# Two-layer decoder trunk: first up weights through the ring of two, an earlier load order where the up phase hands over to the down phase, and two operand or engine changes in attention and output projection

## The chip, the cores and the metric

The kernel runs on one core of a Trainium2 chip. The metric is the device time of one execution in microseconds, the median of several runs. An execution is profiled as well; its trace gives start, duration and releaser of every instruction on each engine: TensorE (PE, matmuls), VectorE (DVE), ScalarE (ACT), GpSimd (POOL) and SyncE (SP, which here only issues DMAs).

## The reference, cut to what matters

```python
for l in range(2):                                   # DEPTH
    h = rms_norm(x, norm1[l]);  proj = h @ w_in[l]   # S = D = 1024, fp32
    a_in, b_in, q, k, v = ...                        # 256 | 512 | 512 | 512 | 512 columns
    ya = pool_mixer(a_in, pool_w[l], pool_scale[l])
    yb = spatial_gate(gelu(b_in), sg_norm[l], sg_w[l], sg_b[l])
    yc = stick_breaking_attention(q, k, v)           # 8 heads of 64
    x = x + concat(ya, yb, yc) @ w_out[l]
    h = rms_norm(x, norm2[l])
    x = x + square(relu(h @ w_up[l])) @ w_down[l]    # 1024 -> 4096 -> 1024
return rms_norm(x, final_norm)

# stick breaking, per query row, causal, with z = q.k / 8
a[j] = sigmoid(z[j]) * prod over j' > j of (1 - sigmoid(z[j']))
out  = a @ v
```

## The kernel before, in words

Activations are kept transposed, as tiles of 128 features by 512 tokens, in two halves of the tokens (c = 1 and 0). Every fp32 product is made of three matmuls on fp32r operands: a value is split into a rounded part h (a cast on ACT, line 155) and a rest l = value - h (a subtraction on DVE, line 156), and h·h, l·h and h·l are added in PSUM (lines 243, 248, 249). In the trace a name such as hT, lT or wh, wl is such a pair.

A layer runs through these stages: input projection with the two small mixers, attention, output projection, up phase, down phase.

**Attention.** For each head and block of 128 queries, `sticks` takes one or two PSUM tiles z of query-key products (ring of three). ACT makes s = sigmoid(-z) (L426) and a = sigmoid(z) (L427), DVE runs a product scan over s in place (L431), and POOL multiplies a by the shifted s (L434). `attend` transposes a on PE, splits the result (L456 on ACT, L458 on DVE) and multiplies with v.

**Output projection.** PE makes 16 outputs `po` per layer. For each, `second` adds the residual on DVE (xa, L870), stores it, and hands the square to POOL's running sum for the norm (L187 on `rbc`). Then `scaled` makes from four outputs the blocks that the up phase multiplies: B11, B21, B22 (h on ACT, l on DVE, L882) and the mixed ones T1 to T4 (t on DVE, L887; h = cast on ACT, L888; l = t - h on POOL, L889).

**Up phase.** The MLP is done by a seven-product scheme on 2x2 blocks (`STEPS`: B11, B21, T2, T1, T3, B22, T4 against A11, A12, S2, S1, S3, S4, A22; PSUM banks X, Y, Z). There are 16 pairs of hidden blocks, `fp`, of seven steps. Each step is 12 matmuls. Its results are relu-squared and written to DRAM: B11 and B21 as finished h/l pairs, the T blocks and B22 raw (`hd_T`, `hd_B`). `weight_steps` brings the next pair's weights: two DMAs of 512 KB into `rt` and `raw` (L823), then splits and sums (`s`, `tmp`, wh, wl, uh, ul, vh, vl). `rt` is a tile of pool `mw`, which is opened after the output projection's pools have closed; `raw` is a ring of two in the pool that lives all the time.

**Down phase.** Groups of two `fp`, each with two halves `u` of seven steps; a step is 2 x 6 matmuls, and every result is added into a tile `acc` on DVE (L1110). A hidden block comes by DMA: finished pairs directly, raw blocks into the ring `hr` of three tiles (L946) followed by a split (L155, L156). At the change of phase the last `fp` steps already load the blocks of group 0 (`b_next`), the rest is loaded in group 0's first steps.

What sets the order: the program is written in Python order and a scheduler that simulates the engines interleaves it. `early(n)` raises priority for evacuations; in the up phase `queue` pins the order on ACT, DVE and POOL to the order of writing. Tile pools with rings make a writer wait for the last reader of the tile it replaces. SP issues DMAs in order, and one whose tile isn't free holds the next ones up.

Of the kernel before, what the change touches and what calls it, by code (L numbers as in the profile page):

```python
# [7 lines left out]
F32 = mybir.dt.float32  # L8
# [6 lines left out]
P = 128  # L15
# [65 lines left out]
def trunk_kernel(tc, xT, w_in, w_out, w_up, w_down, pool_w, sgw, sgb, sgn, cst, outT):  # L81
# [8 lines left out]
    with ExitStack() as ctx:  # L90
# [236 lines left out]
        for l in range(DEPTH):  # L327
# [8 lines left out]
            with (  # L336
# [72 lines left out]
                def sticks(pr, h, i):  # L409

                    c, o = divmod(i, 4)
                    qs = slice(o * P, (o + 1) * P)
                    prev, res = None, {}
                    for kc in ((0, 1) if c == 0 else (1,)):
                        lo = o * P if kc == c else 0
                        w = CH - lo
                        z = ap.tile([P, CH], F32, tag="z", name=nm("z"), bufs=3)
                        kt = kx[pr, h, kc]
                        nc.tensor.matmul(z[:, 0:w], qh[pr, h, c][:, qs], kt[:, lo:CH], start=True, stop=False)
                        mm = nc.tensor.matmul(z[:, 0:w], ql[pr, h, c][:, qs], kt[:, lo:CH], start=False, stop=prev is not None)  # L420
                        if prev is None:
                            mm = nc.tensor.matmul(z[:, 0:P], identr, maskr, start=False, stop=True)
                        last_qk[0] = mm.ins.name
                        s = t512("s", NS, F32, at)
                        a = t512("a", NA, F32, at)
                        nc.scalar.activation(s[:, lo:CH], z[:, 0:w], AF.Sigmoid, scale=-ISQ)  # L426
                        nc.scalar.activation(a[:, lo:CH], z[:, 0:w], AF.Sigmoid, scale=ISQ)  # L427
                        if prev is not None:
                            nc.gpsimd.tensor_mul(a[:, 0:1], a[:, 0:1], prev[:, CH - 1 : CH])
                        sl = s[:, lo:CH]  # L430
                        nc.vector.tensor_tensor_scan(  # L431
                            sl, sl, sl, 1.0 if prev is None else prev[:, CH - 1 : CH], ALU.mult, ALU.bypass
                        )
                        nc.gpsimd.tensor_mul(a[:, lo + 1 : CH], a[:, lo + 1 : CH], s[:, lo : CH - 1])  # L434
                        prev = s
                        res[kc] = a
                    return res
# [359 lines left out]
                b = "T1" if b == "B12" else b  # L797
                return t512("h" + b, 4, F32R, pool), t512("l" + b, 4, F32R, pool)

            def weight_steps(srcs, n, out, eng="pool"):  # L800

# [12 lines left out]
                    return two  # L816

                def load():
                    r["top"] = mw.tile([P, D], F32, tag="rt", name=nm("rt"), bufs=1)
                    r["low"] = per.tile([P, D], F32, tag="raw", name=nm("raw"), bufs=2)  # L820
                    raws = r["top"], r["low"]
                    for raw, src in zip(raws, srcs):
                        nc.sync.dma_start(raw.rearrange("p (f c) -> p f c", f=src.shape[1]), src)  # L823
                    r["a1"], r["a2"] = (x.rearrange(turns, n=n, k=2) for x in raws)
# [42 lines left out]
            def second(m, c, ps):  # L867
# [9 lines left out]
                def scaled(b, src, in1, op):  # L877
# [8 lines left out]
                    t = t512("xt", 3, F32, xs_)  # L886
                    nc.vector.scalar_tensor_tensor(out=t, in0=src, scalar=g, in1=in1, op0=ALU.mult, op1=op)  # L887
                    nc.scalar.copy(h, t)  # L888
                    nc.gpsimd.tensor_sub(lo, t, h.bitcast(F32))  # L889
                    return t  # L890

                if not low and c == 1:
# [45 lines left out]
                acc_[m, c] = pool.tile([P, CH], F32, name=nm("acc"))  # L938
                nc.sync.dma_start(acc_[m, c], xmid[m, c])

            def raw_block(fp, b):

                if b in STORED:
                    return None
                raw = t512("hr", 3, F32, mw)
                nc.sync.dma_start(raw, hid[fp, b])  # L946
                return raw

# [8 lines left out]
                return h, lo  # L957

            a_next = {}
            for step in weight_steps(*up_blocks(0), a_next).values():  # L960
                step()


            with tc.tile_pool(name=f"mu{l}", bufs=1, reuse_waits="tile") as mu:
# [8 lines left out]
                for fp in range(NFP):  # L973
# [51 lines left out]
                    for step in range(len(STEPS)):  # L1025
# [1 line left out]
                        ps = banks[bank]  # L1027
                        b = STEPS[step][3]
                        if (fp, step) == (NFP - 2, 3):
                            raws = {"T2": [raw_block(p, "T2") for p in range(2)], "T1": [raw_block(0, "T1")]}  # L1030
                        if (fp, step) == (NFP - 1, 3):
                            raws["T1"].append(raw_block(1, "T1"))
                        if (fp, step) == (NFP - 1, 4):
                            raws["T3"] = [raw_block(p, "T3") for p in range(2)]
                        if step == 5 and fp == 0:
                            rms(1, 0)
                            rms_done = True
# [27 lines left out]
                        if not classic:  # L1065
# [3 lines left out]
                                mixed("T3", "B22", "B12", nc.vector.tensor_sub)  # L1069
                            elif step == 6:  # L1070
                                mixed("T4", "B21", "T2", nc.vector.tensor_sub)
                        if fp == NFP - 1 and step < 5:
                            for p in range(2):
                                b_next[p][b] = load_block(p, b, raws[b][p] if b in raws else None)
                for k in sorted(left):
# [28 lines left out]
            with tc.tile_pool(name=f"md{l}", bufs=1, reuse_waits="tile") as md:  # L1104
# [8 lines left out]
                for mc in ((3, 0), (2, 1), (3, 1)):  # L1113
# [1 line left out]


                first_acc = {
                    k: [(4 + i + q, c) for q in range(2)] for k, i, c in ((1, 0, 1), (2, 0, 0), (3, 2, 0), (4, 2, 1))
                }
                for g in range(n_groups):  # L1120
                    bs, b_next = b_next, [{}, {}]
                    for u in range(2):
# [6 lines left out]
                        for step in range(len(STEPS)):  # L1129
# [23 lines left out]
                            if g == u == 0:  # L1153
                                for mc in first_acc.get(step, []):
                                    load_acc(*mc, md)
                                if step < 2:
                                    for p in range(2):
                                        bs[p][STEPS[step + 5][3]] = load_block(p, STEPS[step + 5][3])
                            elif g < n_groups - 1:
                                for p in range(2) if g == 0 else (u,):  # L1160
                                    b_next[p][b] = load_block(2 * g + 2 + p, b)
# [122 lines left out]
```

## Time and profile before

| | |
|---|---|
| median of 3 runs | 2274.09 us (2271.59 to 2276.8) |
| the profiled execution's own time | 2273.57 us |
| its span, first to last instruction | 2271.7 us |
| PE busy | 2144.4 us, 94% of the span |
| DVE / POOL / ACT busy | 1830.7 (81%) / 1070.8 (47%) / 952.0 us (42%) |
| mean granted TensorE clock | 0.976 of full speed |
| stages, layer 0 | attention about 40 to 380 us, output projection to 460, up phase to about 803, down phase after that |
| stages, layer 1 | attention about 1160 to 1480 us, up phase from about 1590, down phase from about 1918 |

The page gives an engine's busy time as a sum over its instructions, also where instructions overlap a little in their pipelines. A row of a timeline is one instruction or several alike (xN): start, duration, engine and line, tiles written and read, and in brackets how long the engine had been idle before it and which instruction or DMA ended that. In the table by form, a row is a group of equal instructions with count, busy time and mean ns of one. SPq is the queue of SP, that is, the issue of DMAs.

### The profile page before, as it was taken

How to read it: one execution, taken by the hardware profiler on the slowest of the kernel's cores; microseconds unless marked ns; L12 is line 12 of the kernel's file. 1: busy time of each engine (PE TensorE's matmuls, PEld its weight loads, DVE VectorE, ACT ScalarE, POOL GpSimd, SP SyncE). 2: the span in 40 equal slices, each digit the busy share in tenths (PEclk: the TensorE clock that was granted, in tenths of full speed). 3: DMA queues.
4: the chain of work that ended last, by engine and by line, in shares of the span. 5: the costliest groups of instructions: out<-in, count | busy, mean ns of one | idle time of the engine just before them, and what ended most of it. 6: DMA issues, size and time to landing. Idle time of an engine off the chain costs nothing. (4 is left out here: it accounts for less than half of the span.)

```text
span 2271.7 us, 30343 instructions
## 1 busy us (share of the span) xinstructions
PE 2144.4 (94%) x10608; PEld 1787.6 (79%) x10608; DVE 1830.7 (81%) x2308; ACT 952.0 (42%) x1669; POOL 1070.8 (47%) x851
## 2 busy tenths in 40 slices
PE   7999999979999969999999999997999998999997
PEld 6888897757777758888888888875777776788886
DVE  8788779977777779888868878799677777989864
ACT  5556553443333333333356656435333333333321
POOL 6455556674444433333255646468544444233315
PEclk9999999989999979999999999999999999999998
DMA  3000102235555675554311010133355556755512
GB/s 131 28 29 29 44 25 94 91 117 187 174 176 173 216 261 185 161 192 152 98 52 38 20 47 26 43 93 125 132 182 174 176 174 227 257 190 176 176 43 74
DMA packets 153737, 283.19 MB, mean 125 GB/s; under 512 B 15088, under 2 KB 48368, under 8 KB 153584
## 3 DMA queue, kind: packets, MB, share of 16 engines
q1 hardware_dynamic: 151920, 279.15, 37.2%
q10 hardware_dynamic: 1664, 2.10, 0.3%
q8 instruction: 84, 1.38, 0.2%
q14 instruction: 69, 0.57, 0.1%
HBM read 190.49 MB, written 90.70 MB: 124 GB/s over the span
## 5 line engine op out<-in xcount | busy, mean ns | idle before, releaser
L1000 POOL TENSOR_TENSOR ct<-ct 128x512 f32<-128x512 f32 x128 | 173.8, 1358 | 353.8 <-DVE ct L997 237.3
L434 POOL TENSOR_TENSOR a<-a,s 128x255 f32<-128x255 f32 (+1 forms) x192 | 240.4, 1260 | 181.1 <-ACT a L427 97.0
L836 POOL TENSOR_TENSOR tmp<-rt,raw 128x512 f32<-128x512 f32 x30 | 48.6, 1618 | 344.0 <-DMA rt<-in_w_down 332.1
L243 PE MATMUL pj<-hB,wh 128*128 128x512 f32 x504 | 198.8, 395 | 0.0
L249 PE MATMUL pj<-hB,wl 128*128 128x512 f32 x504 | 197.7, 392 | 0.0
L248 PE MATMUL pj<-lB,wh 128*128 128x512 f32 x504 | 197.7, 392 | 0.0
L1110 DVE TENSOR_TENSOR acc<-acc,po 128x512 f32<-128x512 f32 x240 | 160.6, 679 | 27.4 <-PE po L249 25.3
L991 ACT COPY ct<-po 128x512 f32<-128x512 f32 x66 | 38.8, 588 | 267.0 <-PE po L249 260.5
L155 ACT CAST hT<-hr 128x512 fp32r<-128x512 f32 x122 | 74.9, 620 | 168.4 <-DMA hr<-hd_T 117.4
L458 DVE TENSOR_TENSOR tl<-t,th 128x512 fp32r<-128x512 f32 (+1 forms) x160 | 98.8, 628 | 45.9 <-ACT th L456 44.8
L1012 DVE TENSOR_TENSOR ct<-ct,ct 128x512 f32<-128x512 f32 x120 | 81.3, 699 | 63.0 <-POOL ct L1000 62.0
L431 DVE TENSOR_TENSOR_SCAN s<-s 128x256 f32<-128x256 f32 (+3 forms) x128 | 123.7, 979 | 6.2 <-ACT s L426 5.9
L243 PE MATMUL po<-hB,wh 128*128 128x512 f32 x248 | 99.3, 400 | 26.0 <-ACT wh L155 26.0
L243 PE MATMUL po<-hT,vh 128*128 128x512 f32 x248 | 103.0, 415 | 17.5 <-DVE ct L1054 16.2
L156 DVE TENSOR_TENSOR wl<-rt,wh 128x1024 fp32r<-128x1024 f32 x62 | 110.6, 1784 | 7.1 <-ACT wh L155 7.0
L426 ACT ACTIVATE s<-z 128x256 f32<-128x256 f32 (+1 forms) x192 | 95.4, 500 | 42.9 <-PE z L420 12.3
L243 PE MATMUL po<-hT,wh 128*128 128x512 f32 x256 | 103.1, 403 | 9.8 <-DVE acc L1110 9.7
L243 PEld LDWEIGHTS pj<-hB,wh 128*128 128x128 f32 x504 | 95.3, 189 | 19.7
L248 PEld LDWEIGHTS pj<-lB,wh 128*128 128x128 f32 x504 | 95.3, 189 | 19.7
L249 PEld LDWEIGHTS pj<-hB,wl 128*128 128x128 f32 x504 | 94.9, 188 | 19.9
L156 DVE TENSOR_TENSOR lT<-hr,hT 128x512 fp32r<-128x512 f32 x122 | 97.7, 806 | 14.7 <-ACT hT L155 14.6
L156 DVE TENSOR_TENSOR ct<-ct,ct 128x512 fp32r<-128x512 f32 x64 | 57.2, 893 | 60.0 <-ACT ct L155 60.0
(278 smaller groups left out, 7171.0 us busy)
## 6 DMA issues: line engine op xcount, KB each, us to landing
hd_T<-ct SPq DMA_DIRECT2D x120, 256.0 KB, 2.0
hr<-hd_T SPq DMA_DIRECT2D x120, 256.0 KB, 3.2
raw<-in_w_in SPq DMA_DIRECT2D x36, 512.0 KB, 3.6
raw<-in_w_down SPq DMA_DIRECT2D x34, 512.0 KB, 4.0
raw<-in_w_up SPq DMA_DIRECT2D x32, 512.0 KB, 4.1
rt<-in_w_up SPq DMA_DIRECT2D x32, 512.0 KB, 3.6
rt<-in_w_down SPq DMA_DIRECT2D x30, 512.0 KB, 4.7
hd_B<-ct SPq DMA_DIRECT2D x34, 256.0 KB, 2.0
```

The source lines that it names most:

```text
L155: queue("act", nc.scalar.copy(hi, src))
L156: queue("dve", nc.vector.tensor_sub(lo, src, hi.bitcast(F32)))
L243: mm = nc.tensor.matmul(ps, ah, bh, start=first and i == 0, stop=False, skip_group_check=more)
L248: nc.tensor.matmul(ps, ah, bl, start=False, stop=False, skip_group_check=more)
L249: mm = nc.tensor.matmul(ps, al, bh, start=False, stop=last and i == n - 1, skip_group_check=more)
L426: nc.scalar.activation(s[:, lo:CH], z[:, 0:w], AF.Sigmoid, scale=-ISQ)
L431: nc.vector.tensor_tensor_scan(sl, sl, sl, 1.0 if prev is None else prev[:, CH - 1 : CH], ALU.mult, ALU.bypass)
L434: nc.gpsimd.tensor_mul(a[:, lo + 1 : CH], a[:, lo + 1 : CH], s[:, lo : CH - 1])
L458: nc.vector.tensor_sub(tl[:, 0:wd], pt[:, 0:wd], th[:, 0:wd].bitcast(F32))
L1000: queue("pool", nc.gpsimd.tensor_mul(t, t, t))
L1012: queue("dve", op(t, hb[x], hb[y]))
L1110: (nc.vector.tensor_add if sign > 0 else nc.vector.tensor_sub)(x, x, ps)
```

## The change

Five edits, in the order of the program.

1. **Attention, L431.** The scan's second operand becomes the PSUM tile z in place of s. With the second operation `bypass` its values are not used. The z tile is now read by the scan as well, after both sigmoids.
2. **First up weights.** With `first=True`, `weight_steps` takes both of the first pair's tiles from the ring of two (`raw`), so that the first DMA no longer needs pool `mw`. The second pair's `raw` then waits for a slot of this ring.
3. **Output projection, L889.** l = t - h of T1 to T4 goes from POOL to DVE, 16 subtractions per layer.
4. **Change of phase, loads in the up phase.** T2 and T1 of both pairs of group 0 are loaded at (fp 14, step 3), the second T1 into a tile of the ring `tmp`, since `hr` has only three. Before, that second T1 was loaded at (15, 3) and T3 at (15, 4); T3 is no longer loaded in the up phase, and the last fp prepares blocks in steps 0 to 3 in place of 0 to 4.
5. **Change of phase, loads in the down phase.** In group 0's first half T3, B22 and T4 are loaded at steps 0, 1, 2 (before: B22 and T4 at steps 0, 1), and the `acc` tiles come one step earlier.

```diff
@@ sticks
-                            sl, sl, sl, 1.0 if prev is None else prev[:, CH - 1 : CH], ALU.mult, ALU.bypass
+                            sl, sl, z[:, 0:w], 1.0 if prev is None else prev[:, CH - 1 : CH], ALU.mult, ALU.bypass
@@ weight_steps(srcs, n, out, eng="pool", first=False), load
-                    r["top"] = mw.tile([P, D], F32, tag="rt", name=nm("rt"), bufs=1)
-                    r["low"] = per.tile([P, D], F32, tag="raw", name=nm("raw"), bufs=2)
+                    def low():
+                        return per.tile([P, D], F32, tag="raw", name=nm("raw"), bufs=2)
+
+                    r["top"] = low() if first else mw.tile([P, D], F32, tag="rt", name=nm("rt"), bufs=1)
+                    r["low"] = low()
@@ second, scaled
-                    nc.gpsimd.tensor_sub(lo, t, h.bitcast(F32))
+                    nc.vector.tensor_sub(lo, t, h.bitcast(F32))
@@ raw_block(fp, b, room=None)
-                raw = t512("hr", 3, F32, mw)
+                raw = room or t512("hr", 3, F32, mw)
@@ before the up phase
-            for step in weight_steps(*up_blocks(0), a_next).values():
+            for step in weight_steps(*up_blocks(0), a_next, first=True).values():
@@ up phase
                         if (fp, step) == (NFP - 2, 3):
-                            raws = {"T2": [raw_block(p, "T2") for p in range(2)], "T1": [raw_block(0, "T1")]}
-                        if (fp, step) == (NFP - 1, 3):
-                            raws["T1"].append(raw_block(1, "T1"))
-                        if (fp, step) == (NFP - 1, 4):
-                            raws["T3"] = [raw_block(p, "T3") for p in range(2)]
+                            raws = {b: [raw_block(p, b, p and r and tmp()) for p in range(2)] for b, r in (("T2", 0), ("T1", 1))}
...
-                        if fp == NFP - 1 and step < 5:
+                        if fp == NFP - 1 and step < 4:
                             for p in range(2):
                                 b_next[p][b] = load_block(p, b, raws[b][p] if b in raws else None)
@@ down phase
-                    k: [(4 + i + q, c) for q in range(2)] for k, i, c in ((1, 0, 1), (2, 0, 0), (3, 2, 0), (4, 2, 1))
+                    k: [(4 + i + q, c) for q in range(2)] for k, i, c in ((0, 0, 1), (1, 0, 0), (2, 2, 0), (3, 2, 1))
...
-                                if step < 2:
+                                if step < 3:
                                     for p in range(2):
-                                        bs[p][STEPS[step + 5][3]] = load_block(p, STEPS[step + 5][3])
+                                        bs[p][STEPS[step + 4][3]] = load_block(p, STEPS[step + 4][3])
```

Three places in the order of the engines show what the edits move; lines from L820 up to about L1020 stand four further on in the changed kernel. The first is DVE at the change of phase of layer 0, before. `hr` is a raw hidden block that came by DMA, lT and lB are the rests of its split, `acc` is the down phase's sum.

```order
L156 TENSOR_TENSOR lT_1572_7762<-hr_7572,hT_1571_7761 128x512
L156 TENSOR_TENSOR lT_1574_7766<-hr_7754,hT_1573_7765 128x512
L1054 TENSOR_TENSOR ct_7756<-po_7645,ct_7756 128x512
L997 SCALAR_TENSOR_TENSOR ct_7756<-ct_7756,rbc_5398 128x512
L156 TENSOR_TENSOR wl_7790<-s_1563_7731,wh_7789 128x1024
L156 TENSOR_TENSOR lT_1580_7794<-hr_7781,hT_1579_7793 128x512
L156 TENSOR_TENSOR lT_1582_7798<-hr_7783,hT_1581_7797 128x512
L1058 TENSOR_TENSOR ct_7719<-ct_7719,pg_7647 128x512
L156 TENSOR_TENSOR lB_1606_7892<-hr_7893,hB_1605_7891 128x512
L997 SCALAR_TENSOR_TENSOR ct_7719<-ct_7719,rbc_5398 128x512
L156 TENSOR_TENSOR ul_7817<-tmp_7758,uh_7816 128x512
L156 TENSOR_TENSOR lB_1609_7898<-hr_7899,hB_1608_7897 128x512
```

The same place on DVE after the change:

```order
L156 TENSOR_TENSOR lT_1572_7762<-hr_7572,hT_1571_7761 128x512
L156 TENSOR_TENSOR lT_1574_7766<-tmp_7574,hT_1573_7765 128x512
L1054 TENSOR_TENSOR ct_7756<-po_7647,ct_7756 128x512
L1001 SCALAR_TENSOR_TENSOR ct_7756<-ct_7756,rbc_5398 128x512
L156 TENSOR_TENSOR wl_7786<-s_1564_7733,wh_7785 128x1024
L1058 TENSOR_TENSOR ct_7721<-ct_7721,pg_7649 128x512
L1001 SCALAR_TENSOR_TENSOR ct_7721<-ct_7721,rbc_5398 128x512
L156 TENSOR_TENSOR ul_7805<-tmp_7758,uh_7804 128x512
L156 TENSOR_TENSOR lT_1602_7884<-hr_7885,hT_1601_7883 128x512
L1110 TENSOR_TENSOR acc_7164<-acc_7164,po_7855 128x512
L156 TENSOR_TENSOR lT_1605_7890<-hr_7891,hT_1604_7889 128x512
L1016 TENSOR_TENSOR ct_7808<-ct_7662,ct_7721 128x512
```

The split ahead of L1054 reads a tile that was loaded in fp 14, and the first `acc` follows after one block split of the down phase. Before, five stood ahead of it, four of them in the part shown; the others stand behind the first `acc` now.

The second place is SP around the end of the output projection of layer 0. `xm` is the residual stream written to DRAM, `acc` is the same read back, rt and raw are weights. Before:

```order
L871 DMA xm_0_113<-xa_5157 128x512
L871 DMA xm_1_114<-xa_5184 128x512
L823 DMA rt_5240<-in_w_up 128x1024
L939 DMA acc_7164<-xm_1_100 128x512
L871 DMA xm_0_115<-xa_5207 128x512
```

After:

```order
L875 DMA xm_1_104<-xa_4900 128x512
L827 DMA raw_5240<-in_w_up 128x1024
L875 DMA xm_0_105<-xa_4923 128x512
L875 DMA xm_1_106<-xa_4950 128x512
L875 DMA xm_0_107<-xa_4973 128x512
L827 DMA raw_5241<-in_w_up 128x1024
```

The load of the first pair's upper half moved from behind the fifteenth store of the output projection to behind the fifth.

The third place is PE ahead of the third step of the up phase (the matmuls on hT_1003), layer 0. L198 sums the squares for the norm, L214 transposes the result, pj is bank Y. Before:

```order
L248 MATMUL pj_5270<-lB_1096_5191,wh_5244 128x512
L249 MATMUL pj_5270<-hB_1095_5190,wl_5245 128x512
L198 MATMUL pg_5378<-ones,rbc_4807 128x2 x4
L243 MATMUL po_5269<-hT_1003_4863,wh_5251 128x512
L248 MATMUL po_5269<-lT_1004_4864,wh_5251 128x512
```

After:

```order
L243 MATMUL pj_5270<-hB_1095_5190,wh_5244 128x512
L198 MATMUL pg_5370<-ones,rbc_4785 128x2 x4
L198 MATMUL pg_5378<-ones,rbc_4807 128x2 x4
L248 MATMUL pj_5270<-lB_1096_5191,wh_5244 128x512
L249 MATMUL pj_5270<-hB_1095_5190,wl_5245 128x512
L214 MATMUL pg_5386<-ident,rst_5375 128x128 x4
L214 MATMUL pg_5393<-ident,rst_5383 128x128 x4
L243 MATMUL po_5269<-hT_1003_4863,wh_5251 128x512
```

The transposes of the norm, which came 24 matmuls later, now stand ahead of the third step.

## Rows read from the trace of the kernel before

**Rows 1.** The page's first part: busy time, share of the span, instructions of each engine.

```profile
PE 2144.4 (94%) x10608; PEld 1787.6 (79%) x10608; DVE 1830.7 (81%) x2308; ACT 952.0 (42%) x1669; POOL 1070.8 (47%) x851
```

**Rows 2.** PE's waits, whole span: line, waited for, us in total, times, longest.

```profile
PE po L243 <- ACT wh L155: 26.0, 2, 13.2
PE po L243 <- DVE ct L1054: 16.2, 4, 8.3
PE po L243 <- DVE acc L1110: 9.7, 5, 4.9
PE av L463 <- DVE tl L458: 9.3, 6, 2.8
...
PE pg L243 <- DVE acc L1110: 6.9, 1, 6.9
PE pj L243 <- DVE v L363: 5.8, 3, 2.7
```

**Rows 3.** A stretch of 20 us: its length, busy PE, PEld, DVE, ACT, POOL, clock, DMA share, GB/s.

```profile
820.00:840.00 20.00, 12.17 (x39) 8.89 (x39) 19.17 (x25) 7.38 (x11) 7.07 (x5) 0.76 0.87 299
```

**Rows 4.** Timeline of all engines at layer 0's change of phase.

```profile
796.92 1.77 SPq L946 DMA_DIRECT2D hr<-hd_T  x2
...
802.88 0.62 ACT L155 CAST hT<-hr 128x512 fp32r<-128x512 f32 x1 [8.86 <-DMA hr<-hd_T]
...
803.52 0.69 DVE L156 TENSOR_TENSOR lT<-hr,hT 128x512 fp32r<-128x512 f32 x1 [5.89 <-ACT hT L155]
804.13 0.68 DVE L1054 TENSOR_TENSOR ct<-po,ct 128x512 f32<-128x512 f32 x1
```

**Rows 5.** DVE's timeline after it.

```profile
807.69 3.25 DVE L156 TENSOR_TENSOR lT<-hr,hT 128x512 fp32r<-128x512 f32 x2
...
829.83 1.28 DVE L156 TENSOR_TENSOR lT<-hr,hT 128x512 fp32r<-128x512 f32 x2
...
835.39 3.25 DVE L156 TENSOR_TENSOR lB<-hr,hB 128x512 fp32r<-128x512 f32 x2 [0.75 <-ACT hB L155]
838.56 0.67 DVE L1110 TENSOR_TENSOR acc<-acc,pg 128x512 f32<-128x512 f32 x1
```

**Rows 6.** PE's timeline there.

```profile
804.87 0.79 PE L243 MATMUL po<-hT,vh 128*128 128x512 f32 x1 [8.25 <-DVE ct L1054]
...
818.30 0.47 PE L243 MATMUL po<-hT,wh 128*128 128x512 f32 x1 [3.01 <-DVE acc L1110]
```

**Rows 7.** DVE's timeline at layer 1's change of phase.

```profile
1917.37 0.69 DVE L156 TENSOR_TENSOR lT<-hr,hT 128x512 fp32r<-128x512 f32 x1 [5.46 <-ACT hT L155]
...
1932.71 0.67 DVE L1110 TENSOR_TENSOR acc<-acc,po 128x512 f32<-128x512 f32 x1
```

**Rows 8.** PE's timeline from the last output projection matmul on.

```profile
460.10 0.39 PE L249 MATMUL po<-yh,wl 128*128 128x512 f32 x1
473.26 0.80 PE L243 MATMUL po<-hB,wh 128*128 128x512 f32 x1 [12.77 <-ACT wh L155]
...
478.75 0.79 PE L249 MATMUL po<-hB,wl 128*128 128x512 f32 x1 [2.57 <-DVE wl L156]
...
487.52 0.48 PE L243 MATMUL po<-hT,wh 128*128 128x512 f32 x1
```

**Rows 9.** SP's timeline there.

```profile
467.93 0.37 SPq L823 DMA_DIRECT2D rt<-in_w_up  x1
```

**Rows 10.** DVE's timeline there.

```profile
466.80 1.28 DVE L870 TENSOR_TENSOR xa<-po,hB 128x512 f32<-128x512 f32 x2
```

**Rows 11.** Groups by form, 440 to 468 us: busy, mean ns, idle before.

```profile
L889 POOL TENSOR_TENSOR lT<-xt,hT 128x512 fp32r<-128x512 f32 x9 | 16.1, 1791 | 0.0
L187 POOL TENSOR_TENSOR rbc<-rbc,tmp 128x512 f32<-128x512 f32 x9 | 15.1, 1683 | 0.0
...
L870 DVE TENSOR_TENSOR xa<-po,hB 128x512 f32<-128x512 f32 x7 | 4.7, 677 | 0.0
```

**Rows 12.** Groups by form, whole span.

```profile
L431 DVE TENSOR_TENSOR_SCAN s<-s,s 128x512 f32<-128x512 f32 x64 | 95.4, 1491 | 8.5 <-ACT s L426 6.3
```

More of the change, by code (lines that the diff above doesn't have):

```diff
@@ L798, in block_tiles, with weight_steps @@
                 return t512("h" + b, 4, F32R, pool), t512("l" + b, 4, F32R, pool)
-            def weight_steps(srcs, n, out, eng="pool"):
+            def weight_steps(srcs, n, out, eng="pool", first=False):
                 sub = {"pool": nc.gpsimd, "dve": nc.vector}[eng].tensor_sub
@@ L939, in load_acc, with raw_block @@
                 nc.sync.dma_start(acc_[m, c], xmid[m, c])
-            def raw_block(fp, b):
+            def raw_block(fp, b, room=None):
                 if b in STORED:
                     return None
-                raw = t512("hr", 3, F32, mw)
+                raw = room or t512("hr", 3, F32, mw)
                 nc.sync.dma_start(raw, hid[fp, b])
```

## Prediction

> **What bounds the kernel now.** I read the page's busy times first. PE is busy for 2144.4 of 2271.7 us [rows 1], so about 127 us of the span are PE's idle time, and an edit to other engines can only win a part of that. Next I read what PE waits for over the whole span: a few places make most of it [rows 2]. Twice it waits 13 us at L243 for wh, at the start of the two up phases (26.0). At the two changes from up to down phase it waits for `ct` of L1054 (16.2 in all, the longest 8.3) and for `acc` of L1110 (6.9 at bank Z; 9.7 in five waits on po, the longest 4.9). Attention's largest are behind tl (9.3) and v (5.8). The third view was stretches of 20 us: in 820 to 840 us PE is busy for 12.17 us at a clock of 0.76 while DVE is busy for 19.17 [rows 3]. There DVE is the bound; elsewhere in the long phases PE is. Last I read the timelines at the two kinds of place.
>
> At layer 0's change of phase SP issues two loads of `hr` at 796.92, ACT starts the cast of the second T1 block at 802.88 after waiting 8.86 us for such a DMA, DVE has been idle for 5.89 us when it can split that block, and L1054 comes only behind that split on DVE's queue [rows 4]. PE waits 8.25 us for L1054 [rows 6], though L1054 itself needs nothing of the block. Then DVE is full of splits, and PE waits for `acc` at 818.30 (3.01 us) [rows 6] and behind the one of 838.56, which two splits of 3.25 us delayed [rows 5].
>
> At the start of the up phase the last output matmul starts at 460.10 and the first up matmul at 473.26, after 12.77 us of waiting for ACT's wh, then 2.57 for wl [rows 8]. The cause is the load: `rt` is issued at 467.93 [rows 9], because its pool opens late.
>
> **The change, part by part.** *Change of phase.* The second T1 now comes from a load in fp 14, more than a whole fp earlier, so the split ahead of L1054 finds it there. The idle times that end in this split go: 5.89 in layer 0 [rows 4], 5.46 in layer 1 [rows 7], together 11.3. T3's loads leave the stretch in front of the change, and its splits, like those of B22 and T4, now come in group 0, between the evacuations. In layer 0 four splits of the next group stood ahead of the `acc` on which PE waited for 6.9 us; two cost 1.28 and two 3.25 [rows 5], so 4.5 go from that wait. In layer 1 five splits stood ahead of the first `acc`, in the 15.3 us from 1917.37 to 1932.71 [rows 7]; one stands there now, and I take PE's wait of 4.9 [rows 2] as gone. For layer 0's 3.01 I take nothing: DVE has no free time there, and what moves behind one `acc` is ahead of the next. Sum: 11.3 + 4.5 + 4.9 = 20.7. Bounds: if all deferred work comes back as waits, layer 0 gains nothing (DVE is the bound to 840) and layer 1 keeps its 5.5. If all goes, it is 11.3 + 3.0 + 6.9 + 4.9 = 26.1. The `acc` loads one step earlier cost SP ten issues in another place; they are covered by seven steps of PE work.
>
> *First up weights.* The upper half is issued behind the fifth store of the output projection in place of the fifteenth, so wh and wl are there when the output projection ends. SP's stores behind it wait only if a ring slot isn't free, and both are, since no other weights are loaded between. What is late next is DVE. Its last two xa take 466.80 to 468.08 [rows 10]; behind them, up to the split lT of T2 that the third step needs, stand eleven operations of 512 columns, two of 1024 (wl, vl) and two tiny ones. DVE starts the next one after 0.61 when undisturbed (803.52 to 804.13 [rows 4]) and about 1.62 when POOL is at work (two in 3.25 [rows 5]). POOL has about four operations left there, 4 x 1.7 = 7 us by its rows [rows 11], which cover four of the eleven. The rest is 7 x 0.61 and 2 x 1.2, so lT comes at 468.1 + 7 + 6.7 = 481.8. The third step begins ten matmuls earlier, but the norm's transposes, which wait for a short chain over DVE and POOL, now stand ahead of it: I take 481 against 487.52 before [rows 8], a gain of 6.5 per layer, 13 in all. Bounds: undisturbed 13 x 0.61 + 1.2 = 9.1, hence lT at 477.2 and a start at 475, 12.5 per layer; contended throughout, 13 x 1.62 + 1.6 = 22.7, lT at 490.8 and a start at 488.5, a loss of 1 per layer. The second pair's `raw` now waits for the first's slot, with later weights queued behind it on SP; it isn't needed for six further steps, more than 16 us, which cover it.
>
> *Subtraction on DVE.* In the output projection POOL is the bound: L889 and L187 alternate without a gap, 1791 and 1683 ns [rows 11], 13.7 us for each four outputs (four of each). Without L889 POOL needs 6.7. DVE then has, per four outputs, fifteen operations of 0.61 and about four stretched by one more us each, 9.2 + 4 = 13.2. So the bound passes to DVE at almost the same pace, and I book 0; in the worst case one more is stretched in each four, 4 us per layer.
>
> *Attention.* The scan now reads one operand from SBUF and one from PSUM. xa, with one operand in PSUM, takes 677 ns [rows 11] though POOL is busy all the time beside it, while scans of the same size take 1491 [rows 12], and the two-input splits were stretched from 0.69 [rows 4] to over 1.6 [rows 5]. I expect shorter scans and shorter POOL multiplications, though both engines are off the path for most of attention. The waits for tl and v, 15.1 together [rows 2], are the most that can go. On the other side z is held until the scan's end. I book -2, between -15 and +12 (the second is the rival below, on some 14 tiles).
>
> The rows show no price for an operand in PSUM: an addition that reads it takes 0.67 [rows 5], a subtraction in SBUF alone 0.69 [rows 4]. [...]
>
> Sum against the profiled execution: 2273.6 - 20.7 - 13 - 2 = 2237.9. The profiled execution lies 0.5 below the median of the runs, so the same sum from the median is 2238.4; I take 2238.
>
> **The rivals.** (1) The waits only move: T3, B22 and T4 are fetched in group 0, where DVE is full, and PE waits for them in steps 4 to 6 instead. For it: DVE's 19.17 of 20 [rows 3]. Against it: the loads start in step 0, four steps before use, and five splits have left the path of the first `acc`. Gain 5.5 in place of 20.7: 2273.6 - 5.5 - 13 - 2 = 2253.
>
> (2) DVE becomes the bound where the up phase starts, through 16 more subtractions: the third step starts where it did or 1 us later. For it: fifteen operations behind the last xa. Against it: POOL, which stretches them, has half its work left. 2273.6 - 20.7 + 2 - 2 = 2253.
>
> (3) Slower: the z ring. A z tile is freed by the scan's end in place of the second sigmoid's. A scan takes 1.49 [rows 12], an ACT pass over such a tile 0.62 [rows 4], so a slot comes free up to 0.9 later, and PE, with three slots, may stand for it before the next product. It decides from 36 / 0.9 = 40 of the 192 tiles on; at the 64 full chained scans it costs 57.6: 2273.6 - 35.7 + 57.6 = 2295. Against it: PE has transposes and products of other blocks between.
>
> (4) Attention gains all of its 15.1: 2273.6 - 20.7 - 13 - 15.1 = 2225. For it: tl and v stand behind scans on DVE's queue.
>
> (5) Each scan pays more to start with an operand in PSUM. Start-up hidden by the overlap of two operations can be 0.06 (durations of 0.67, starts 0.61 apart [rows 4, 5]): 192 x 0.06 = 11.5, if all on the path, 2273.6 - 33.7 + 11.5 = 2251. [...]
>
> That the change doesn't do what it says I leave out: the order has the loads and splits where the diff puts them.
>
> **How the numbers follow.** Forecast 0.46; (1) 0.18; (2) 0.13; (3) 0.08; (4) 0.12; (5) 0.03. The likeliest one's own range is 2228 to 2248. To 8 in 10 the range takes in (1), (2) and (5) and part of (4), with some room for (1) and (2) together (2268): 2220 to 2262. A measurement of this kernel can tell about 0.2%, 4.5 us, from no change. Slower is (3) with most of its weight, 0.08; within 0.2% are (1) and (2) together with a few held z tiles, 0.05; faster is the rest, 0.87.
>
> **What would show it.** Right: at the change of phase no DMA ends DVE's idle time ahead of L1054, and PE waits there under 3 us; PE's wait for wh at the up phase's start falls from 12.8 to under 2, and the third step starts near 481; scans of 512 columns average under 1.35 us; POOL has no gapless stretch before the up phase. Wrong: new waits of PE for lT or lB in group 0 of the down phase; DVE gapless to beyond 485 us; waits of PE for z behind the scan; a total gain from one of the two kinds of place alone.

## The result, and the profile after

The changed kernel takes 2242.57 us (median of 4 runs, 2241.48 to 2247.47) against 2275.14 for the kernel before (4 runs, 2271.59 to 2276.8): ratio 0.9864, 95% interval 0.9848 to 0.9881. That is 31 us less; the forecast was 2238. The profiled execution is the longest of the four, 2247.47 with a span of 2244.8.

The starts of four kinds of instructions in the timeline cut the profiled spans into stages. "Steady up phase" is the start of the 457th product matmul (lines 243, 248, 249), counted from the up phase's third step; from there on both kernels run at the same pace, 0.234 us from one product matmul to the next over 800 of them. By this cut attention ends at 348.0 us in layer 0 of the kernel before, earlier than the rough 380 given for it above. The last column is the change of PE's idle time in the stage, its length less its busy time.

| stage, us | before, layer 0 / 1 | after, layer 0 / 1 | change | forecast | PE's idle time |
|---|---|---|---|---|---|
| attention: first z to first output matmul | 304.9 / 296.7 | 298.6 / 294.4 | -8.6 | -2 | -13.2 |
| output projection and up start: to steady up phase | 248.8 / 248.9 | 245.3 / 245.1 | -7.4 | -13 | -2.4 |
| change of phase: to the down phase's last addition, its end | 546.4 / 494.8 | 539.3 / 487.0 | -14.9 | -20.7 | -10.5 |
| rest (start, between the layers, end) | 131.2 | 135.2 | +3.9 | 0 | +0.6 |

The rest is this one execution's: 2.75 of it is a later first z, whose start varies from 43.1 to 45.9 us between executions of kernels that are the same up to there. The first two stages don't hold the same work in both kernels: in the changed one 24 matmuls per layer, which stood among the output projection's before, are done within attention. So PE's idle time, which is what the forecast booked, shows more than the lengths: attention gave 11.2 more than forecast, the other two terms 10.6 and 10.2 less. That the sum came within 5 us of the forecast is luck in large part.

The page's first row after, to be held against [rows 1]:

```profile
PE 2143.0 (95%) x10608; PEld 1782.6 (79%) x10608; DVE 1792.2 (80%) x2340; ACT 950.6 (42%) x1669; POOL 959.4 (43%) x819
```

PE has the same work. GpSimd is busy for 111 us less and VectorE for 39 less, though VectorE has 32 instructions more. What PE waits for, whole span, against [rows 2]:

```profile
PE po L243 <- DVE acc L1110: 10.1, 9, 3.1
PE pg L214 <- POOL rst L204: 9.7, 5, 2.9
PE po L243 <- DVE xa L874: 8.1, 8, 1.8
PE po L248 <- DVE lB L886: 7.8, 2, 3.9
PE pg L243 <- DVE acc L1110: 7.2, 2, 6.4
...
PE po L243 <- DVE ct L1054: 4.8, 4, 2.4
PE z L419 <- DVE s L431: 4.3, 6, 1.0
...
PE av L463 <- DVE tl L458: 2.6, 2, 1.3
...
PE pj L243 <- DVE v L363: 0.4, 1, 0.4
```

The 26.0 for wh are gone and in their place stand new or longer waits, most of them at the same place in the program: rst, xa, lB. L1054 fell from 16.2 to 4.8. The 6.9 for `acc` at bank Z is a 6.4 still. In attention tl and v fell from 15.1 to 3.0. The z ring costs 4.3, for the scan; before, it cost 3.0, for the second sigmoid, a wait that is gone:

```profile
PE z L419 <- ACT a L427: 3.0, 5, 0.8
```

At the change of phase of layer 0, VectorE and then PE, against [rows 4 to 6]:

```profile
790.57 0.68 DVE L156 TENSOR_TENSOR lT<-tmp,hT 128x512 fp32r<-128x512 f32 x1
791.17 0.68 DVE L1054 TENSOR_TENSOR ct<-po,ct 128x512 f32<-128x512 f32 x1
...
798.25 0.68 DVE L1110 TENSOR_TENSOR acc<-acc,po 128x512 f32<-128x512 f32 x1
...
820.55 1.18 DVE L156 TENSOR_TENSOR lT<-hr,hT 128x512 fp32r<-128x512 f32 x1 [1.86 <-ACT hT L155]
821.65 0.68 DVE L1110 TENSOR_TENSOR acc<-acc,pg 128x512 f32<-128x512 f32 x1
```

```profile
791.91 0.50 PE L243 MATMUL po<-hT,vh 128*128 128x512 f32 x1 [2.36 <-DVE ct L1054]
...
809.96 0.47 PE L243 MATMUL po<-hT,uh 128*128 128x512 f32 x1 [3.11 <-DVE acc L1110]
...
822.38 0.79 PE L243 MATMUL pg<-hB,vh 128*128 128x512 f32 x1 [6.38 <-DVE acc L1110]
```

The split ahead of L1054 has no idle time before it any more. But PE still stands for 6.38 us at bank Z, and VectorE is idle for 1.86 of it: this is not the full queue that the forecast saw there. In layer 1 the waits are 0.58 and under 1 us, and its first `acc` starts 7.6 us after L1054 (1899.67 and 1892.04) in place of 14.7 [rows 7].

PE around the start of the up phase, against [rows 8]:

```profile
453.29 0.39 PE L249 MATMUL po<-yh,wl 128*128 128x512 f32 x1
455.42 0.47 PE L243 MATMUL po<-hB,wh 128*128 128x512 f32 x1 [1.75 <-DVE xa L874]
...
461.83 0.50 PE L248 MATMUL po<-lB,wh 128*128 128x512 f32 x1 [3.88 <-DVE lB L886]
...
475.04 2.08 PE L214 MATMUL pg<-ident,rst 128*128 128x128 f32 x8 [2.86 <-POOL rst L204]
478.58 2.08 PE L214 MATMUL pg<-ident,rst 128*128 128x128 f32 x8 [1.46 <-POOL rst L204]
480.31 0.77 PE L243 MATMUL po<-hT,wh 128*128 128x512 f32 x1
```

The first up matmul follows the last output matmul by 2.1 us where it was 13.2. The third step begins at 480.31, nearly the 481 of the forecast, but the output projection now ends 6.8 us earlier: from its end to the third step it is 26.6 us, before 27.0. VectorE in that stretch, its last addition of the residual and the splits ahead of the third step:

```profile
463.57 0.68 DVE L874 TENSOR_TENSOR xa<-po,hB 128x512 f32<-128x512 f32 x1
...
477.57 2.95 DVE L893 TENSOR_TENSOR lT<-xt,hT 128x512 fp32r<-128x512 f32 x3
```

### The profile page after: what moved, and what is told of

It is laid out like the page before. It is cut to its first block, busy times and chain, and to the rows that moved or that the text cites. A ratio compares the mean times of both kernels' runs of the same rounds, so it can differ in the third digit from the quotient of the medians.

```text
span 2244.8 us, 30340 instructions
## 1 busy us (share of the span) xinstructions
PE 2143.0 (95%) x10608; PEld 1782.6 (79%) x10608; DVE 1792.2 (80%) x2340; ACT 950.6 (42%) x1669; POOL 959.4 (43%) x819
## 5 line engine op out<-in xcount | busy, mean ns | idle before, releaser
L434 POOL TENSOR_TENSOR a<-a,s 128x255 f32<-128x255 f32 (+1 forms) x192 | 199.8, 1045 | 232.2 <-DVE s L431 216.7
L431 DVE TENSOR_TENSOR_SCAN s<-s,z 128x256 f32<-128x256 f32 (+3 forms) x128 | 103.2, 811 | 28.7 <-ACT a L427 27.0
L156 DVE TENSOR_TENSOR wl<-rt,wh 128x1024 fp32r<-128x1024 f32 x60 | 106.0, 1767 | 11.9 <-ACT wh L155 11.9
L243 PE MATMUL po<-yh,wh 128*128 128x512 f32 x256 | 100.9, 402 | 9.8 <-ACT yh L155 5.2
L833 POOL TENSOR_TENSOR s<-raw 128x512 f32<-128x512 f32 x62 | 91.5, 1476 | 33.7 <-DVE wl L156 24.3
```

Source lines behind the costliest of these rows:

```text
L156: queue("dve", nc.vector.tensor_sub(lo, src, hi.bitcast(F32)))
L243: mm = nc.tensor.matmul(ps, ah, bh, start=first and i == 0, stop=False, skip_group_check=more)
L431: nc.vector.tensor_tensor_scan(sl, sl, z[:, 0:w], 1.0 if prev is None else prev[:, CH - 1 : CH], ALU.mult, ALU.bypass)
L833: queue("pool", nc.gpsimd.tensor_add(s1, r["a2"][:, 0], r["a2"][:, 1]))
```

## The experiments

The ratio is to the kernel before, timed beside the run; intervals are 95%.

| run | what it is | median, us | ratio to before |
|---|---|---|---|
| e1_scan | before + scan's operand | 2261.77 | 0.9937 (0.9924 to 0.9951) |
| e2_sub | before + subtractions on VectorE | 2266.05 | 0.9959 (0.9945 to 0.9973) |
| e3_first | before + first weights early | 2273.90 | 0.9989 (0.9979 to 0.9998) |
| e4_loads | before + both load orders | 2259.31 | 0.9930 (0.9915 to 0.9944) |
| e5_no_sub | changed - subtractions | 2249.83 | 0.9880 (0.9863 to 0.9897) |
| e6_t1 | before + second T1 in fp 14 | 2269.70 | 0.9965 (0.9951 to 0.9980) |
| e7_behind | changed + next group's splits later | 2242.85 | 0.9847 (0.9829 to 0.9865) |
| e8_half | changed, T3 and T4 on GpSimd | 2247.64 | 0.9870 (0.9852 to 0.9887) |
| e9_tile | e7_behind + one `acc` tile early | 2240.40 | 0.9850 (0.9835 to 0.9864) |
| e10_no_first | changed - first weights early | 2246.44 | 0.9875 (0.9860 to 0.9890) |
| e11_rest_pool | changed, first rests on GpSimd | 2245.13 | 0.9870 (0.9853 to 0.9887) |
| e12_norm | e9_tile + norm behind third step | 2242.53 | 0.9863 (0.9841 to 0.9886) |

**e1_scan**: only the first hunk of the diff. 

> The kernel before with the scan's second operand from PSUM alone. Theory (the scan and GpSimd stop getting in each other's way, and the waits of PE behind tl and v in attention shrink; the trace of the changed kernel has first z to first output matmul 6.3 us shorter in layer 0 and 2.2 in layer 1): -8.5 us, about 2265, with the 512-column scans near 1.28 us. Rival 1 (attention is off the path, what the trace of the changed kernel shows there comes from the other edits' reordering): within 2 us of before. Rival 2 (the z ring holds PE up): slower, with waits of PE for the scan of more than 10 us.

It gained 14 us by the ratio, more than expected; in its trace attention is 10.2 us shorter over the two layers. PE's idle time there fell by 14.3, from 21.2 to 6.9; 24 matmuls more per layer are done in it, and the output projection, where they are missing, is no shorter for it (112.0 and 112.5 us against 112.1 and 112.2). The scans by line (ns, min/median/max) and the multiplications, before, and then the multiplications, scans and waits in e1_scan:

```profile
L431 DVE TENSOR_TENSOR_SCAN s<-s,s x64: 1254/1284/2218, 61.6 to 1428.7; 128x512 f32<-128x512 f32 x64
...
L434 POOL TENSOR_TENSOR a<-a,s 128x511 f32<-128x511 f32 x96 | 138.9, 1447 | 55.8 <-ACT a L427 26.2 <-DVE s L431 23.6 <-DVE tl L458 1.8
```

```profile
L434 POOL TENSOR_TENSOR a<-a,s 128x511 f32<-128x511 f32 x96 | 126.3, 1316 | 115.2 <-DVE s L431 114.9
...
L431 DVE TENSOR_TENSOR_SCAN s<-s,s,z 128x512 f32<-128x512 f32 x64 | 81.7, 1276 | 8.4 <-ACT a L427 2.7 <-issue 1.4 <-POOL a L434 0.9
```

```profile
PE z L419 <- DVE s L431: 3.2, 5, 0.9
...
PE av L463 <- DVE tl L458: 2.6, 2, 1.3
```

The mean scan fell from 1491 [rows 12] to 1276 and GpSimd's multiplication from 1447 to 1316. That isn't because the two engines no longer meet: in the changed kernel, which has the same scan, 44 of the 96 scans of 512 columns overlap GpSimd's instructions for more than half of their time, and none takes more than 1.28 us. In the kernel before 68 overlap so, and they take 1.45 us in the mean and up to 2.22; the 12 that overlap for less than a twentieth take 1.28 at most. The z ring costs 3.2 us in five waits for the scan, where it had cost 3.0 in five for the second sigmoid: the slower rival's mechanism is there, but it adds next to nothing, and not 57.6. The rest of the 14 lies outside attention, mostly in the change of phase (5.3 shorter), where the interval (3 us either way) and moved schedules can't be told apart.

**e2_sub**: only the third hunk. 

> The kernel before with the 16 subtractions per layer on VectorE alone. Theory (GpSimd bounds the output projection before; VectorE bounds it after, at a little better pace): the output projection 3.25 us shorter per layer as in the trace of the changed kernel, and nothing at the start of the up phase, where the weights still come late: -6.5 us, about 2267. Rival (VectorE's longer queue ends later, so that the third step of the up phase starts later by what the projection gained): 0.

9 us by the ratio, neither the theory's place nor the rival's 0: the output projection itself is 0.3 us shorter per layer. To steady up phase it is 2.9 and 2.2 us. The rest stands in other stages, whose order the scheduler had changed too.

**e3_first**: only the edits of `weight_steps`. 

> The kernel before with the first up weights in the ring of two alone; GpSimd keeps the subtractions. Theory (in the changed kernel it is VectorE's queue, with the 16 subtractions in it, that holds the third step of the up phase 26.6 us behind the output projection's end; with the subtractions on GpSimd the weights' gain comes out): from the end of the output projection to the third step some 20 us in place of 27, -6.5 per layer, -13 in all, about 2261. Rival (GpSimd's or VectorE's queue holds the third step anyway, also without the 16 subtractions): 24 us or more there, -1 to -6 in all.

The theory fell; the size is the rival's. The third step comes 4.1 us earlier (23.0 after the output projection in place of 27.0), and 2 of that are lost again by steady up phase. The rows of PE:

```profile
476.53 1.87 PE L198 MATMUL pg<-ones,rbc 128*128 128x2 f32 x8 [2.60 <-POOL rbc L187]
...
479.87 1.87 PE L198 MATMUL pg<-ones,rbc 128*128 128x2 f32 x8 [1.48 <-POOL rbc L187]
...
483.75 0.79 PE L243 MATMUL po<-hT,wh 128*128 128x512 f32 x1 [2.01 <-ACT ct L994]
```

With the subtractions on GpSimd, its sum of squares `rbc` is late, and the norm stands ahead of the third step on PE.

**e4_loads**: only the edits at the change of phase. 

> The kernel before with the two load orders at the change of phase alone. Theory (from the trace of the changed kernel: third step of the up phase to the last addition of the down phase 7.1 us shorter in layer 0 and 7.9 in layer 1): -15 us, about 2259, with one stall of about 6 us for an addition left in layer 0's first group, behind the split of a block of the next group. Rival (the 20.7 of the prediction is there when the other edits don't shift the loads): -20 or more, without that stall.

15.6 us by the medians, the theory's number, with the same wait of 6.4 for `acc` at bank Z. So this part is nearly independent of the others.

**e5_no_sub** and **e10_no_first**: the changed kernel with one part undone. 

> The changed kernel with the subtractions t - h back on GpSimd. Alone, moving them gained 0.41% (9 us). Theory (with the weights there early, the output projection's end and the third step of the up phase are set by whichever of VectorE and GpSimd has the longer queue, and either of the two lengths is nearly the same): from the last output matmul to steady up phase it gets a little better and the output projection 3 us worse per layer, in all 2 to 5 us slower than the changed kernel, about 2246. Rival (the gain of the move is its own whatever the weights do): 9 us slower, about 2252.

> The changed kernel without the first up weights in the ring of two (they come through rt again). Alone, that edit gained 0.11% (1 to 4 us). Theory (VectorE's queue sets the third step whether the weights are early or not, so that the edit is worth little here too): 1 to 4 us slower than the changed kernel, about 2245, with PE's 12 us wait for wh back and the waits for lB, rbc and rst gone. Rival (together with the other edits it is worth what was predicted): 13 us slower, about 2255.

The medians lie near both theories' numbers. By the ratios 3.6 and 2.5 us are lost against the changed kernel, but its interval overlaps both, so that a loss of nothing can't be ruled out. The rival's 9 for e5_no_sub lies at the edge of the intervals, the rival's 13 for e10_no_first outside. In the traces the stage from the first output matmul to steady up phase is 3.3 and 4.1 us longer than in the changed kernel without the subtractions, and 2.0 and 3.8 longer without the early weights. In e10_no_first PE waits 12.3 us at the old place, but for the squares, no longer for wh:

```profile
PE pg L198 <- POOL rbc L187: 12.3, 2, 10.2
```

The weights would have held PE nearly as long: ACT's cast of wh ends at 464.38 there, and the first up matmul starts at 464.44, right behind these column sums.

**e8_half**, **e11_rest_pool**, **e12_norm**: what holds the up phase's start?

```diff
-                    nc.vector.tensor_sub(lo, t, h.bitcast(F32))
+                    (nc.gpsimd if b in ("T3", "T4") else nc.vector).tensor_sub(lo, t, h.bitcast(F32))   # e8_half
...
+            if pool:                       # e11_rest_pool: split(..., first) of the first weights
+                nc.gpsimd.tensor_sub(lo, src, hi.bitcast(F32))
...
+        # e12_norm: add_manual_dep(op.ins, third) on the matmuls of L198 and L214, third = the third step's last
```

> The changed kernel with the subtractions of T3 and T4 back on GpSimd, those of T1 and T2 left on VectorE. Theory (VectorE's queue, gapless for 40 us up to the third step, sets when the up phase starts; eight subtractions less per layer are 5 to 7 us less of it, and GpSimd has a third of its time free there): third step 3 to 6 us earlier after the output projection in each layer, -6 to -12 us, about 2234. Rival (the norm's chain over GpSimd, which stands ahead of the third step on PE, holds it whatever VectorE does): within 2 us of the changed kernel.

> The changed kernel with the rests of the first pair's weights (wl twice, ul, vl, once per layer) made by GpSimd in place of VectorE. Theory (VectorE's gapless queue sets the third step): some 4 us less of that queue per layer, the third step 2 to 5 us earlier after the output projection, -4 to -10 us, about 2236. Rival (GpSimd's part, the sum of squares and the norm's chain, holds the third step and now has 8 us more to do): same or up to 10 us slower.

> e9_tile with the norm's matmuls on PE (the column sums and the transposes, which stood ahead of the third step of the up phase) ordered behind that step's last matmul. Theory (in the changed kernel PE stood 1.5 us for rbc, 2.9 and 1.5 us for rst ahead of the third step, while the split that this step needs was ready at the same time; neither VectorE's 8 subtractions nor the weights' rests moved it, so the norm's chain over ScalarE, GpSimd and VectorE is what holds it): the third step starts 3 to 6 us earlier after the output projection, -4 to -10 us, about 2234. Rival (VectorE's queue up to lT is as long as the norm's chain, so PE waits inside the third step instead; or the first relu, which needs the norm, is late next): within 2 us of e9_tile.

None gained. e8_half has the third step 23.0 and 24.5 us after the output projection, in place of 26.6, nearly as its theory had it, but the projection is 6.4 and 4.7 us longer than in the changed kernel. In e11_rest_pool PE waits for lB and rst where it waited before (4.9, 2.9, 3.0). In e12_norm the third step starts 3.4 us nearer to the projection's end than in e9_tile, at 474.91, and then the first relu lacks the norm, so that `ct` tiles and banks come free late:

```profile
474.91 0.79 PE L258 MATMUL po<-hT,wh 128*128 128x512 f32 x1 [3.77 <-ACT ct L1010]
...
505.68 0.51 PE L258 MATMUL po<-hT,uh 128*128 128x512 f32 x1 [0.53 <-ACT ct L1010]
...
511.58 0.53 PE L258 MATMUL pg<-hB,vh 128*128 128x512 f32 x1 [2.86 <-ACT ct L1010]
```

From the first output matmul to steady up phase it takes 4 to 5 us more than e9_tile. So it is not one engine's queue alone. A reading that fits all three: scaling, splits, squares and norm of 16 outputs share VectorE and GpSimd, and whatever is put first, another of them is late. It is argued, not shown; a version that takes work away from this stage wasn't tried.

**e6_t1**: one thing of the change of phase.

```diff
-                            raws = {"T2": [raw_block(p, "T2") for p in range(2)], "T1": [raw_block(0, "T1")]}
-                        if (fp, step) == (NFP - 1, 3):
-                            raws["T1"].append(raw_block(1, "T1"))
+                            raws = {b: [raw_block(p, b, p and r and tmp()) for p in range(2)] for b, r in (("T2", 0), ("T1", 1))}
```

> The kernel before with only one thing of the change of phase: the second T1 block is loaded in fp 14 into a tile of the ring tmp; T3's loads and splits stay where they were. Theory (in layer 0 VectorE is the bound up to the end of the first half of group 0, so the vanished wait of 5.9 us comes back as later waits for additions; in layer 1 about 5 of its 5.5 us stay): -4 to -8 us, about 2269, with the wait for L1054 under 3 us and longer waits for acc. Rival (the vanished waits are gained in full): -11.3, about 2263.5.

The size was right, the place was not. L1054's waits fell to 2.36 and 0.56, but of the change of phase layer 0 keeps 5.5 us and layer 1 only 0.4. PE in layer 1:

```profile
1927.64 0.47 PE L243 MATMUL po<-hT,uh 128*128 128x512 f32 x1 [3.38 <-DVE acc L1108]
...
1938.47 0.79 PE L243 MATMUL pg<-hB,vh 128*128 128x512 f32 x1 [4.88 <-DVE acc L1108]
```

So in layer 1 most of the removed wait comes back behind `acc`, while layer 0 keeps nearly all of its 5.9: the reverse of the theory. With the other changes of load order too, e4_loads keeps 8.1 and 7.5; which of them frees layer 1 wasn't taken apart.

**e7_behind** and **e9_tile**: the stall that was left.

```diff
+                tc.add_manual_dep(op.ins, behind[0], ...)   # e7_behind: these splits after the first half's last acc
-                early_acc += [(q, 1 - u) for q in range(2)] + [(2, 0)] * u
+                early_acc += [(q, 1 - u) for q in range(2)] + [(2, 0), (3, 0)] * u   # e9_tile
```

> The changed kernel with VectorE's splits of the next group's blocks T1, T3, B22 and T4 (those that group 0's second half loads) ordered behind the last addition of group 0's first half. Theory (the stall of 6.4 us in layer 0 stands behind the split of such a block, which waits for a transfer under way, not behind work that VectorE must do): the stall goes, -4 to -8 us, about 2237. Rival (VectorE has no free time, the deferred splits only hold later additions up): within 2 us of the changed kernel.

> e7_behind, and the down phase's tile acc (3, 0), on whose first addition PE waited there, is loaded with the early tiles in fp 12 (one more tile in the pool mw) in place of at the change of phase. Theory (in e7_behind the addition itself waited 2.35 us for the load of its tile, which SP issues behind the next group's blocks): the wait of 5.1 us for an addition in layer 0 falls under 2.5, 3 to 5 us faster than e7_behind, about 2239 against the changed kernel's 2242.6. Rival (the tiles (2, 1) and (3, 1), loaded at the same place, are late next): the stall moves by one step, within 1 us.

In e7_behind the split is gone from its place and PE still waits; the time is the rival's, within 2 us of the changed kernel. VectorE and PE there:

```profile
819.06 0.69 DVE L1118 TENSOR_TENSOR acc<-acc,pg 128x512 f32<-128x512 f32 x1 [2.35 <-DMA acc<-xm]
...
819.80 0.79 PE L250 MATMUL pg<-hB,vh 128*128 128x512 f32 x1 [5.12 <-DVE acc L1118]
```

The addition waits for its own tile, whose load lands at 819.03. In the changed kernel too that load, the first `acc<-xm` here, stands on SP behind a block of the next group; it lands at 820.5, and the addition starts at 821.65:

```profile
814.59 0.32 SPq L950 DMA_DIRECT2D hr<-hd_T  x1
815.00 0.94 SPq L943 DMA_DIRECT2D acc<-xm  x2
```

With the tile loaded early, PE in e9_tile:

```profile
817.99 0.47 PE L250 MATMUL po<-hT,vh 128*128 128x512 f32 x1 [0.81 <-DVE acc L1118]
...
860.64 0.50 PE L250 MATMUL po<-hT,vh 128*128 128x512 f32 x1 [2.03 <-DVE acc L1118]
```

The stall is gone, and from the third step on layer 0 keeps 12.9 us in place of 7.1 (17 at first; 4 are lost again up to the end of group 1's first half, where VectorE is busy for 37.2 of 37.3 us). By the times e9_tile is 2 us faster than the changed kernel and its interval overlaps, so that it is a better version is likely and not shown. The early tile without e7_behind's order wasn't run.

## Why the prediction came out, point by point

**Change of phase, 20.7 forecast, 14.9 measured (15.6 alone).** Right: the wait in front of L1054, the two 11.3, and a first `acc` without five splits ahead: from the third step of the up phase to the first `acc` both layers are 12 us shorter. The step that failed is "so 4.5 go from that wait": the wait of 6.9 was put down to four splits that cost 1.28 and 3.25. e7_behind and e9_tile show that behind them stood the tile's own load, queued on SP; the splits were only the last thing ahead of it. The kernel before has the same limit:

```profile
831.50 6.81 SPq L939 DMA_DIRECT2D acc<-xm  x11
```

The first of these loads is this tile's and lands 5.2 us later, at 836.7; the addition starts at 838.56 [rows 5], so the splits cost it 1.9 at most. Rival 1 (waits move into group 0) was right in part: about 5 us of the 12 come back in each layer, in layer 1 as waits for `acc`, and e6_t1 shows how much when only one wait is removed.

The sum also booked waits alone. Of the 14.9, 10.5 is idle time of PE and 4.4 is busy time, for the same number of matmuls. What differs is the clock. In the kernel before, after PE stood for 8.25 us, the granted clock is 0.50 of full speed from 805.0 to 808.5, and matmuls start 0.43 us apart; from 809.5 to 814.0 it is 1.00 and they start 0.23 apart. In these stages 66 matmuls of the kernel before start 0.40 to 0.46 us ahead of the next, and 33 after the change.

**First up weights, 13 forecast; 0.4 per layer from the projection's end to the third step.** The wait for wh vanished as forecast and the third step stood where I put it, 480.3 against 481, but that is luck. The step that failed is the base of "a gain of 6.5 per layer": it kept the last xa's end at 468.08 and set 481 against the old 487.52, while the output projection now ends 6.8 us earlier, 3.6 through attention and 3.3 through its own length, with 24 matmuls less in it. VectorE, with the 16 subtractions, ends its last xa only 3.8 earlier, at 464.25, which is 10.6 us behind the projection's end in place of 7.6. The queue behind it was forecast well: its eleventh operation of 512 columns, the first of the three splits at 477.57, ends 14.0 us later (13.7 in the forecast). The third step starts 2.1 after that, behind the norm's transposes, whose chain the forecast had called short: PE waits 2.86 and 1.46 for rst. Alone the edit is worth 0.11%, in the changed kernel by the ratios about as much (e10_no_first). Rival 2 had the right outcome. Its mechanism, VectorE alone, isn't the whole: e8_half and e11_rest_pool unload VectorE for nothing.

**Subtraction on VectorE, 0 booked.** By the ratios 9.3 us alone and 3.6 in the changed kernel, with intervals too wide to tell these apart. The forecast put this term at nothing, though its rows give 13.9 us of GpSimd for each four outputs (4 x 1791 + 4 x 1683 ns; it has 13.7), 0.7 more than its 13.2 for VectorE. The bound did pass on to VectorE, which is busy without a gap from 440 to 480 us. Alone the edit shortens the output projection by 0.3 us only; undone in the changed kernel it makes it 3.6 and 2.0 longer. What I missed besides is that GpSimd's squares end earlier, at 468.7 in place of 475.9 us in layer 0, and with them the norm. How much of the gain is due to that isn't shown.

**Attention, -2 booked, -8.6 measured.** Mechanism right, size wrong: I took it that both engines are off the path for most of attention, while 12.1 of the 15.1 for tl and v could go (rival 4), and the z ring's waits rose only from 3.0 to 4.3 (rival 3). PE's idle time in the stage fell by 13.2; the length shows less, since the 24 matmuls per layer moved into it. The chained scans no longer vary:

```profile
L431 DVE TENSOR_TENSOR_SCAN s<-s,s,z x64: 1261/1279/1282, 67.1 to 1407.7; 128x512 f32<-128x512 f32 x64
```

The longest fell from 2218 ns to 1282, and GpSimd's multiplication in the mean from 1447 to 1303. Why an operand from PSUM does this, no run takes apart. Rival 5's 0.06 us more for each scan with an operand in PSUM doesn't show: the shortest chained scan is 1261 ns against 1254, 7 more.

All the signs of being right came, and one of being wrong, the waits for z behind the scan. Still each of the three terms is off by more than 5 us: such signs tell that the places changed, not what that is worth.

## What to carry to other kernels

A wait has a last cause and others close behind it: before booking one as gone, look at what the waiting instruction itself needs, its own operand's load included, and at what that load is queued behind. Where several engines share a stage's work, as ahead of the up phase here, an early operand alone mostly moved the wait (e3_first gained 0.11%); whether less work in the stage would help wasn't tried. A stage that is cut at instructions can change its work when the order changes, so compare the idle time of the engine that bounds it, and count its instructions. Where a VectorE instruction has an operand that isn't used, try one from PSUM: here the chained scan's mean fell from 1491 to 1276 ns and that of GpSimd's multiplication beside it from 1447 to 1316 (e1_scan).

## What the runs showed that was not expected

The parts don't add up: alone they gain 14.3, 9.3, 2.5 and 15.9 us by their ratios (scan, subtractions, first weights, load orders), 42 in all, together 31. Edits that touch no instruction of a stage move it through the scheduler all the same: e2_sub's layer 0 is 3.5 us shorter from steady up phase to the first `acc`, where nothing was edited.
